# Moving odd-sized tiles to the front of SBUF in a two-layer decoder trunk, so that the streamed tiles start at multiples of 512 bytes

## Chip, cores, metric

One core of a Trainium2 chip runs the whole program. The metric is device time in microseconds from one execution to the next of the same kernel; lower is better.

## What is computed

Two decoder layers on 256 positions of width 2048, all in float32. A layer mixes tokens by two branches that run side by side, adds the result to x, then adds an MLP and a gated per-layer embedding. Cut to what matters:

```python
u = rms_norm(x, g_mix[l])
cq_raw, ckv_raw, xb, yb, gate_a, gate_r = split_columns(u @ w_in[l])
attn = mla_branch(cq_raw, ckv_raw, ...)   # low-rank q and kv, 16 heads, causal softmax
rec = rglru_branch(xb, yb, ...)           # conv of 4 taps, gates by 128x128 blocks, linear scan, gelu(yb) gate
merged = sigmoid(gate_a) * attn + sigmoid(gate_r) * rec
x = x + merged @ w_out[l]
x = x + square(relu(rms_norm(x, g_mlp[l]) @ w_up[l])) @ w_down[l]
x = x + sigmoid(rms_norm(x, g_ple[l]) @ w_ple_gate[l]) * (p[l] @ w_ple_proj[l])
# after both layers: rms_norm(x, g_final)
```

## The kernel before

Everything is kept transposed: features on the 128 partitions, the 256 positions along the free axis. A float32 product is made of three float32r products: each operand is split into a rounded part (hi) and the rest (lo), and TensorE runs hi x hi, hi x lo and lo x hi. So each 128x128 weight tile is worth three matmuls that stream 256 columns.

Weights come from HBM in halves of 128 x 1024 floats, 502 a layer, in the order in which they are used. `load` (line 139) fetches one into a `raw` buffer (six of them), up to eight halves ahead; `split_half` (line 155) has ScalarE write `hi` (line 160) and VectorE write `lo` (line 164), three buffers of each, two halves ahead. Activations are split in the same way: `bufA` and `bufB` hold 16 feature tiles x (hi, lo) x 256 positions, and take turns as input and output of the stages.

TensorE's work is issued by a few helpers. `mm3` (line 257) issues the three products of one weight tile: lines 259, 260 and 261. `mm_both` (line 274) issues a half for two output tiles at once, 24 matmuls, all at line 284; four halves, 96 matmuls, make a pair of output tiles (`mm_pair`). In the trace a matmul is named output <- streamed tile, weight tile: `up<-bufA,hi`.

A layer runs c (compressed q and kv, 8 halves a pair of inputs), kr (rope key, by `mm3` on bufA or bufB), then eight groups of two heads: xb, yb, (in group 0: gr), k, v, q, qr, lru, (from group 1: gr), ga. k, q and qr stream `c1hi`, `c1lo`, `c0hi`, `c0lo`; lru streams the split convolution output; v has c1 as the stationary side and streams `hi` and `lo`. Between the pieces of gr and ga, and of the next group's xb, small blocks run: scores s (lines 259 to 261 and 984), transposes pt (lines 1017 to 1019) and values o (line 1040, on `v` and `pt_hi`, `pt_lo`). Then come out, four chunks of up and down, and pg, with pp (the per-layer embedding's projection) between. The norm's sums (`ms`, line 555) and its spreading (`rb`, line 604) are small matmuls behind the first pieces of a stage.

The order on each engine is set by a planner that runs while the program is built: `work` chooses vector and scalar steps by estimated costs, and `half` and the helpers add up TensorE's time. It knows neither addresses nor pools.

Addresses in SBUF follow from the pools: a pool takes its place behind the pool opened before it, and within one a tile takes its place behind the tile made before it, each rounded up to 32 bytes. The first free byte of a partition is 16,512 (128 past a multiple of 512). Before, `const` comes first, with `x`, `bufA`, `bufB` and then small tiles among large ones; `wraw`, `wsp`, `tmp`, `att` and `tiny` follow.

Of the kernel before, what the change touches and what calls it, by code (L numbers as in the profile page):

```python
# [11 lines left out]
F32 = mybir.dt.float32  # L12
# [6 lines left out]
P = 128  # L19
S = 256  # L20
D = 2048
KT = D // P
DEPTH = 2
# [21 lines left out]
NPC = _c  # L45
# [8 lines left out]
def _parts(x, bits, n):  # L54

    out = []
    x = Fraction(x)
    for i in range(n):
        if x == 0:
            out.append(0.0)  # L60
            continue
        b = bits if i < n - 1 else 24
        m, e = math.frexp(float(x))
        q = Fraction(2) ** (e - b)
        v = Fraction(round(x / q)) * q
        out.append(float(v))
        x -= v
    return out


def _centered(x):
    x = x - math.floor(x)
    return x - 1 if x > Fraction(1, 2) else x
# [3 lines left out]
def trunk_kernel(ctx: ExitStack, tc: tile.TileContext, xT, pT, pos, par, gfin, invf, wu, out):  # L77
    nc = tc.nc

    const = ctx.enter_context(tc.tile_pool(name="const", bufs=1))  # L80
    wraw = ctx.enter_context(tc.tile_pool(name="wraw", bufs=6))
    wsp = ctx.enter_context(tc.tile_pool(name="wsp", bufs=3))
    tmp = ctx.enter_context(tc.tile_pool(name="tmp", bufs=6))
    att = ctx.enter_context(tc.tile_pool(name="att", bufs=1))
    tiny = ctx.enter_context(tc.tile_pool(name="tiny", bufs=4))
    banks = {
        t: (ctx.enter_context(tc.tile_pool(name=f"ps_{t}", bufs=n, space=PSUM)), n)
        for t, n in (("mm", 3), ("s", 2), ("t", 1), ("o", 1), ("r", 1))
# [120 lines left out]
    def later(key, *steps, deps=(), rank=1, also=()):  # L209

        job = Job((key, *also), rank, deps, steps)
        at = len(jobs)
        while at and jobs[at - 1].rank > rank:
            at -= 1
        jobs.insert(at, job)
# [126 lines left out]
        return tmp.tile([P, S], F32, tag="h", bufs=3, name=name)  # L342


    x = const.tile([P, KT, S], F32, name="x")

    bufA, bufB = (const.tile([P, KT, 2, S], F32R, name=n) for n in ("bufA", "bufB"))
    parT = const.tile([P, DEPTH * NPC], F32, name="parT")
    gf = const.tile([P, KT], F32, name="gf")
    nc.sync.dma_start(out=parT, in_=par)  # L350
    nc.sync.dma_start(out=x[:, 0:2, :], in_=xT[:, 0:2, :])
    load_to(0)
# [12 lines left out]
    make_identity(nc, ident)  # L365
    ones = const.tile([P, P], F32, name="ones")
    V.memset(ones, 1.0)
    power = const.tile([P, 4], F32, name="power")
    A.activation(power, ones[:, 0:4], AF.Copy, scale=-0.5)
    mask = const.tile([P, S], F32, name="mask")  # L370
    V.memset(mask[:, 0:P], 0.0)
# [2 lines left out]
    ropeS = const.tile([P, S], F32, name="ropeS")  # L374

    def rope_tables():
        fr = const.tile([P, 1], F32, name="invf")
        nc.sync.dma_start(out=fr, in_=invf)
        slots = []
        for n, tag in enumerate(("xch", "xcl", "vh", "vl")):  # L380
            w = att.tile([P, 512], F32, tag=tag, name=f"rope_w{n}")
            slots += [w[:, 0:S], w[:, S:512]]
        posi, ang, p2, p1, rem, turn, k, k2 = slots
        nc.sync.dma_start(out=posi.bitcast(I32), in_=pos.partition_broadcast(P))
        ops = []

        def ts(*a, **kw):
            ops.append(("V", 0.21, lambda: V.tensor_scalar(*a, **kw)))

        def tt(*a, **kw):  # L390
            ops.append(("V", 0.35, lambda: V.tensor_tensor(*a, **kw)))

        def rounded(o, src, by):
            ts(out=o, in0=src, scalar1=by, scalar2=ROUND, op0=ALU.mult, op1=ALU.add)
            ts(out=o, in0=o, scalar1=ROUND, scalar2=None, op0=ALU.subtract)

        def less(o, src, kk, c):
            ops.append(("V", 0.35, lambda: V.scalar_tensor_tensor(out=o, in0=kk, scalar=-c, in1=src, op0=ALU.mult, op1=ALU.add)))

        ops.append(("V", 0.21, lambda: V.tensor_copy(ang, posi.bitcast(I32))))  # L400
        ts(out=ang, in0=ang, scalar1=fr, scalar2=None, op0=ALU.mult)

        rounded(p2, ang, 2.0 ** -20)
        less(rem, ang, p2, 2.0 ** 20)
        rounded(p1, rem, 2.0 ** -10)
        less(rem, rem, p1, 2.0 ** 10)
        for n, (p, e) in enumerate(((p2, 20), (p1, 10))):
            c = _parts(_centered(Fraction(2) ** e / (2 * _PI)), 12, 3)
            if n == 0:
                ts(out=turn, in0=p, scalar1=c[0], scalar2=None, op0=ALU.mult)  # L410
            else:
                less(turn, turn, p, -c[0])
            rounded(k, turn, 1.0)
            less(turn, turn, k, 1.0)
            less(turn, turn, p, -c[1])
            less(turn, turn, p, -c[2])
        rounded(k, turn, 1.0)
        less(turn, turn, k, 1.0)
        c = _parts(2 * _PI, 12, 3)
        rounded(k2, rem, float(1 / (2 * _PI)))  # L420
        for v in c:
            less(rem, rem, k2, v)
        less(rem, rem, turn, -float(2 * _PI))
        rounded(k, rem, float(1 / (2 * _PI)))
        for v in c:
            less(rem, rem, k, v)
        ts(out=k, in0=rem, scalar1=3.1415925, scalar2=-3.1415925, op0=ALU.min, op1=ALU.max)

        ts(out=k2, in0=k, scalar1=-1.0, scalar2=None, op0=ALU.mult)
        tt(out=k2, in0=k, in1=k2, op=ALU.max)  # L430
        ts(out=k2, in0=k2, scalar1=-1.0, scalar2=math.pi / 2, op0=ALU.mult, op1=ALU.add)
        ops.append(("A", 1.0, lambda: A.activation(ropeS, k, AF.Sin)))
        ops.append(("A", 1.0, lambda: A.activation(ropeC, k2, AF.Sin)))

        for b in (0, 64):
            ts(out=ropeS[b:b + 32, :], in0=ropeS[b:b + 32, :], scalar1=-1.0, scalar2=None, op0=ALU.mult)
        later("rope", *ops, rank=1)


    cl = const.tile([P, DEPTH, 16], F32, name="cl")  # L440
    cl2 = const.tile([P, DEPTH, 16], F32, name="cl2")
    hba = const.tile([P, DEPTH, 16], F32, name="hba")
    hbx = const.tile([P, DEPTH, 16], F32, name="hbx")

    def lru_constants():
        work_ = t512("lru_c")
# [196 lines left out]

    PT = tuple(att.tile([P, 512], F32R, name=f"pt_{w}") for w in ("hi", "lo"))

    xbuf = att.tile([P, 2, 260], F32, name="xbuf")
    V.memset(xbuf[:, :, 0:4], 0.0)

    def split_steps(d, name, src, tag, cols=512):
# [35 lines left out]
    def mixer(l, u, mg, norm):  # L685
# [9 lines left out]
        for n in range(4):  # L695
            i, pr = divmod(n, 2)
            key = ("c", i, pr, l)
            ps = mm_pair(f"c{i}{pr}_{l}", key, u, hooks.get(n, ()))
            later(key, ("A", 0.6, lambda i=i, pr=pr, ps=ps: A.activation(dest(i, pr), ps, AF.Copy)), rank=-1)
            if l == n == 0:  # L700
                rope_tables()
                lru_constants()
            nl.squares((nl.name, "sq", n), lambda i=i, pr=pr: raw[i, pr], i, deps=(key,), last=pr == 1)
# [729 lines left out]
```

## Time and profile before

| | us |
|---|---|
| median of 3 runs | 2882.05 (2879.41 to 2883.55) |
| profiled execution | 2881.91 |
| its span, first to last instruction | 2880.1 |
| TensorE busy | 2853.1 (99%) |
| VectorE busy | 1861.3 (65%) |
| ScalarE busy | 1538.4 (53%) |
| DMA queues, share of 16 engines | 56.1% |

The span lies 1.8 us under the execution's own time. TensorE's share says that it is never long without a matmul, not how fast one follows another: the recorded ends of matmuls are modelled and overlap their successors. The distance from start to start, or a piece of the chain of waits divided by its count, gives the pace.

### The profile page before, as it was taken

The page shows a single profiled execution, that of the slowest core. Times are in us where ns is not written, and L with a number is a line of the kernel's source. Part 1 is how long each engine was busy: PE and PEld are TensorE (multiplying, and loading weights), DVE is VectorE, ACT ScalarE, POOL GpSimd, SP SyncE. Part 2 cuts the span into 40 slices and gives each one's busy share as a digit, 9 for nine tenths or more (in the row PEclk, how much of TensorE's full clock was granted, in tenths as well). Part 3 has the DMA queues.
Part 4 walks back from the last instruction along what each step waited for, and adds up shares of the span by engine and source line. Part 5 has one row for each costly group of instructions (what it writes and reads, how often), then busy time and mean ns, then how long its engine had stood idle before and what let it go on. Part 6 is the DMA issues. An engine that isn't in the chain of part 4 may idle for free.

```text
span 2880.1 us, 60564 instructions
## 1 busy us (share of the span) xinstructions
PE 2853.1 (99%) x24800; PEld 2846.8 (99%) x24800; DVE 1861.3 (65%) x2420; ACT 1538.4 (53%) x2050; POOL 10.1 (0%) x17
## 2 busy tenths in 40 slices
PE   8999999999999999999999999999999999999998
PEld 8999999999999999999999999999999999999998
DVE  7877777765555555556758777777555555555665
ACT  5666666644444443444546666666453444434555
POOL 0000000000000000000000000000000000000000
PEclk9999999999999999999999999999999999999999
DMA  6555555555555555655555555555555555555553
GB/s 232 169 176 179 172 171 178 178 184 190 197 193 194 195 193 195 198 195 191 190 188 172 176 169 176 176 178 179 186 191 195 194 196 193 194 194 197 196 187 129
DMA packets 272583, 535.43 MB, mean 186 GB/s; under 512 B 30512, under 2 KB 30768, under 8 KB 272304
## 3 DMA queue, kind: packets, MB, share of 16 engines
q1 hardware_dynamic: 272304, 531.55, 55.6%
q8 instruction: 194, 3.18, 0.4%
q14 instruction: 85, 0.70, 0.1%
HBM read 529.33 MB, written 2.10 MB: 185 GB/s over the span
## 4 chain that ended last, share of the span: by engine, by line
PE 98%; ACT 1%; DVE 0%; DMA 0%; issue 0%; SPq 0%; ACTq 0%; POOLq 0%
PE up L284 24%; PE down L284 21%; PE yb L284 6%; PE gr L284 6%; PE xb L284 6%; PE out L284 5%; PE pg L284 5%; PE ga L284 5%; PE c L284 3%; PE down L259 1%; PE down L260 1%; PE down L261 1%; PE o L1040 1%; PE s L984 1%; PE v L872 1%; PE v L873 1%
## 5 line engine op out<-in xcount | busy, mean ns | idle before, releaser
L160 ACT ACTIVATE hi<-raw 128x1024 fp32r<-128x1024 f32 x1004 | 1065.7, 1061 | 1311.6 <-DMA raw<-wu 467.4
L164 DVE TENSOR_TENSOR lo<-raw,hi 128x1024 fp32r<-128x1024 f32 x1004 | 1229.5, 1225 | 808.1 <-ACT hi L160 786.0
L284 PE MATMUL up<-bufA,hi 128*128 128x256 f32 x2048 | 316.2, 276 | 0.0
L284 PE MATMUL up<-bufB,hi 128*128 128x256 f32 x2048 | 316.2, 276 | 0.0
L284 PE MATMUL down<-bufB,hi 128*128 128x256 f32 x1792 | 276.0, 276 | 0.0
L284 PE MATMUL down<-bufA,hi 128*128 128x256 f32 x1792 | 276.0, 276 | 0.0
L284 PEld LDWEIGHTS up<-bufA,hi 128*128 128x128 f32 x2048 | 270.6, 188 | 0.1
L284 PEld LDWEIGHTS up<-bufB,hi 128*128 128x128 f32 x2048 | 270.6, 188 | 0.1
L284 PEld LDWEIGHTS down<-bufB,hi 128*128 128x128 f32 x1792 | 236.4, 188 | 0.0
L284 PEld LDWEIGHTS down<-bufA,hi 128*128 128x128 f32 x1792 | 236.4, 188 | 0.0
L284 PE MATMUL up<-bufA,lo 128*128 128x256 f32 x1024 | 199.7, 276 | 0.0
L284 PE MATMUL up<-bufB,lo 128*128 128x256 f32 x1024 | 199.6, 276 | 0.0
L284 PE MATMUL down<-bufA,lo 128*128 128x256 f32 x896 | 174.5, 276 | 0.0
L284 PE MATMUL down<-bufB,lo 128*128 128x256 f32 x896 | 174.4, 276 | 0.0
L284 PEld LDWEIGHTS up<-bufA,lo 128*128 128x128 f32 x1024 | 154.4, 188 | 0.0
L284 PEld LDWEIGHTS up<-bufB,lo 128*128 128x128 f32 x1024 | 154.3, 188 | 0.0
L284 PEld LDWEIGHTS down<-bufA,lo 128*128 128x128 f32 x896 | 134.9, 188 | 0.0
L284 PEld LDWEIGHTS down<-bufB,lo 128*128 128x128 f32 x896 | 134.8, 188 | 0.0
L284 PE MATMUL xb<-bufB,hi 128*128 128x256 f32 x512 | 81.4, 281 | 0.0
L284 PE MATMUL yb<-bufB,hi 128*128 128x256 f32 x512 | 81.3, 281 | 0.0
L284 PE MATMUL yb<-bufA,hi 128*128 128x256 f32 x512 | 81.3, 281 | 0.0
L284 PE MATMUL xb<-bufA,hi 128*128 128x256 f32 x512 | 81.3, 281 | 0.0
(563 smaller groups left out, 5630.8 us busy)
## 6 DMA issues: line engine op xcount, KB each, us to landing
raw<-wu SPq DMA_DIRECT2D x1744, 256.0 KB, 3.0
raw<-wu SPq DMA_DIRECT2D x132, 512.0 KB, 3.3
y<-rows SPq DMA_DIRECT2D x4, 512.0 KB, 4.0
x<-xT SPq DMA_DIRECT2D x3, 512.0 KB, 7.5
x<-xT SPq DMA_DIRECT2D x2, 256.0 KB, 4.3
praw<-pT SPq DMA_DIRECT2D x2, 256.0 KB, 4.0
parT<-par SPq DMA_DIRECT2D x1, 184.0 KB, 2.5
rope_w<-pos SPq DMA_DIRECT2D x1, 128.0 KB, 4.4
```

What stands on the lines that cost most here:

```text
L160: A.activation(hi, src, AF.Copy)
L164: V.tensor_tensor(out=lo, in0=src, in1=f(hi), op=ALU.subtract)
L259: T.matmul(o, lhsT=wh, rhs=ah, start=start, stop=False, skip_group_check=shared)
L260: T.matmul(o, lhsT=wh, rhs=al, start=False, stop=False, skip_group_check=shared)
L261: T.matmul(o, lhsT=wl, rhs=ah, start=False, stop=stop, skip_group_check=shared)
L284: T.matmul(ps[:, t * S:(t + 1) * S], lhsT=w[:, (4 * t + kk) * P:(4 * t + kk + 1) * P], rhs=a, start=k == n == t == 0, stop=k == 15 and n = ...
L872: T.matmul(o, lhsT=ch, rhs=wh, start=k == 0, stop=False)
L873: T.matmul(o, lhsT=ch, rhs=wl, start=False, stop=False)
L984: T.matmul(o, lhsT=qr, rhs=kr["rot"][w][:, 0:n], start=False, stop=m == 1)
L1040: T.matmul(o[:, j * P:S], lhsT=v[:, j * S + t * P:j * S + (t + 1) * P], rhs=q[:, c], start=n == 0, stop=n == 5, skip_group_check=True,)
```

## The change

Two pools are opened ahead of the others, `small` and `even`, and `tiny` is moved between them. The parameter tiles, `gf`, `power`, `invf`, `cl`, `cl2`, `hba`, `hbx` and the convolution's input `xbuf` go from `const` and `att` to `small`. `even` holds one tile of 32 bytes that nothing uses.

```diff
+    small = ctx.enter_context(tc.tile_pool(name="small", bufs=1))
+    tiny = ctx.enter_context(tc.tile_pool(name="tiny", bufs=4))
+    even = ctx.enter_context(tc.tile_pool(name="even", bufs=1))
     const = ctx.enter_context(tc.tile_pool(name="const", bufs=1))
...
-    tiny = ctx.enter_context(tc.tile_pool(name="tiny", bufs=4))
...
+    even.tile([P, 8], F32, name="even")
     x = const.tile([P, KT, S], F32, name="x")
...
-    parT = const.tile([P, DEPTH * NPC], F32, name="parT")
-    gf = const.tile([P, KT], F32, name="gf")
+    parT = small.tile([P, DEPTH * NPC], F32, name="parT")
+    gf = small.tile([P, KT], F32, name="gf")
...
-    power = const.tile([P, 4], F32, name="power")
+    power = small.tile([P, 4], F32, name="power")
...
-        fr = const.tile([P, 1], F32, name="invf")
+        fr = small.tile([P, 1], F32, name="invf")
...
-    cl = const.tile([P, DEPTH, 16], F32, name="cl")
...
+    cl = small.tile([P, DEPTH, 16], F32, name="cl")
...
-    xbuf = att.tile([P, 2, 260], F32, name="xbuf")
+    xbuf = small.tile([P, 2, 260], F32, name="xbuf")
```

`cl2`, `hba` and `hbx` change as `cl` does. The two programs have the same instructions in the same order, with the same waits, on all five engines. What differs is where tiles begin, in bytes of a partition, and the remainder by 512:

| tiles | before | rest | after | rest |
|---|---|---|---|---|
| x | 16,512 | 128 | 20,992 | 0 |
| bufA, bufB | 32,896; 65,664 | 128 | 37,376; 70,144 | 0 |
| ident, ones | 99,968; 100,480 | 128 | 102,912; 103,424 | 0 |
| mask, ropeC, ropeS | from 101,024 | 160 | from 103,936 | 0 |
| norm sums, R | from 104,640 | 192 | from 107,008 | 0 |
| raw (6), hi (3), lo (3) | from 109,760 | 192 | from 112,128 | 0 |
| tmp tiles, pt_hi, pt_lo | from 158,912 | 192 | from 161,280 | 0 |
| xbuf | 178,368 | 192 | 18,592 | 160 |
| other att tiles: xc, v, q, k, c0, c1, kr, qs, p, rec | from 180,448 | 224 | from 180,736 | 0 |
| small tiles, tiny | 98,432 to 104,608; 228,576 | various | 16,512 to 20,960 | various |

Each streamed tile's size is a multiple of 512 bytes; a 128-column weight slice is 512 bytes, a row of bufA 1,024. So the slices of a tile have the tile's remainder. The last byte in use goes from 228,832 to 228,864.

## Rows read from the trace of the kernel before

**Rows 1.** The page's parts 1, 2 and 4: engines, granted clock, chain that ended last.

```profile
PE 2853.1 (99%) x24800; PEld 2846.8 (99%) x24800; DVE 1861.3 (65%) x2420; ACT 1538.4 (53%) x2050; POOL 10.1 (0%) x17
...
PEclk9999999999999999999999999999999999999999
...
PE 98%; ACT 1%; DVE 0%; DMA 0%; issue 0%; SPq 0%; ACTq 0%; POOLq 0%
```

**Rows 2.** The longest pieces of the chain: start us, us, what it was.

```profile
78.82 10.89 PE yb L284 x96
...
140.57 11.31 PE yb L284 x96
163.12 8.18 PE gr L284 x72
...
551.45 79.15 PE out L284 x672
641.91 11.31 PE up L284 x96
...
730.60 76.16 PE down L284 x672
817.64 87.04 PE up L284 x768
...
1926.10 11.31 PE yb L284 x96
```

**Rows 3.** Busy time and granted clock in four stretches: out, down, yb, gr.

```profile
core 0: us, PE busy (x) PEld busy (x) DVE busy (x) ACT busy (x) POOL busy (x), PEclk, DMA share, GB/s
560.00:640.00 80.00, 80.00 (x682) 80.00 (x681) 48.73 (x56) 39.80 (x50) 0.00 (x0) 1.00 0.56 186
740.00:800.00 60.00, 60.00 (x532) 60.00 (x531) 31.26 (x29) 23.39 (x22) 0.00 (x0) 1.00 0.59 195
201.00:212.00 11.00, 11.00 (x95) 11.00 (x95) 8.49 (x12) 5.48 (x7) 0.00 (x0) 1.00 0.58 193
90.00:100.00 10.00, 10.00 (x91) 10.00 (x90) 9.14 (x15) 5.54 (x7) 0.00 (x0) 1.00 0.57 194
```

**Rows 4.** The chain in shorter stretches, 60 to 70 and 137 to 176 us.

```profile
60.43 0.11 PE kr L259
...
65.87 2.72 PE xb L284 x24
...
137.69 2.88 PE xb L284 x24
...
151.88 0.12 PE k L259
...
163.00 0.12 PE lru L261
...
171.29 0.12 PE s L259
...
171.88 0.06 PE s L259
171.94 0.12 PE s L260
172.06 0.11 PE s L261
172.17 0.22 PE s L984 x2
172.39 2.79 PE gr L284 x24
```

**Rows 5.** TensorE's instructions in order of time: start us, us, what, tiles, count.

```profile
start us, us, engine line op out<-in xcount [idle before <-releaser]
...
68.43 0.95 PE L555 MATMUL ms_c<-ones,nacc_c 128*128 128x1 f32 x8
69.23 0.72 PE L284 MATMUL xb<-bufA,hi 128*128 128x256 f32 x4
69.79 0.40 PE L284 MATMUL xb<-bufA,lo 128*128 128x256 f32 x2
...
137.30 0.40 PE L1040 MATMUL o<-pt_lo,v_0h 128*128 128x256 f32 x2
137.53 0.68 PE L284 MATMUL xb<-bufA,hi 128*128 128x256 f32 x4
138.05 0.40 PE L284 MATMUL xb<-bufA,lo 128*128 128x256 f32 x2
```

**Rows 6.** Vector steps of lines 785 and 637 (duration ns min/median/max); who waited, us, times, longest.

```profile
L785 DVE SCALAR_TENSOR_TENSOR xc<-xbuf,parT,xc x96: 475/479/482, 92.4 to 1931.4; 128x256 f32<-128x256 f32 x96
...
L637 DVE SCALAR_TENSOR_TENSOR bufA<-x,parT,bufA x48: 476/480/485, 5.0 to 1342.4; 128x256 fp32r<-128x256 f32 x48
...
ACT hi L160 <- DMA raw<-wu: 467.4, 284, 2.2
...
PE c L284 <- ACT hi L160: 8.6, 1, 8.6
```

More of the change, by code (lines that the diff above doesn't have):

```diff
@@ L437, in rope_tables @@
         later("rope", *ops, rank=1)
-    cl = const.tile([P, DEPTH, 16], F32, name="cl")
-    cl2 = const.tile([P, DEPTH, 16], F32, name="cl2")
-    hba = const.tile([P, DEPTH, 16], F32, name="hba")
-    hbx = const.tile([P, DEPTH, 16], F32, name="hbx")
+    cl = small.tile([P, DEPTH, 16], F32, name="cl")
+    cl2 = small.tile([P, DEPTH, 16], F32, name="cl2")
+    hba = small.tile([P, DEPTH, 16], F32, name="hba")
+    hbx = small.tile([P, DEPTH, 16], F32, name="hbx")
     def lru_constants():
```

## The prediction

> **What bounds the kernel now.** I read the page first: TensorE is busy 99% of the span, its granted clock is full in all 40 slices, and 98% of the chain that ended last is TensorE [rows 1]. The other engines can be late only where TensorE waits for them, and it hardly does. So the question is at what pace TensorE goes from one matmul to the next; for that I read the chain piece by piece and divide a piece's length by its count. Nearly all of the 24,800 matmuls have one form: a 128x128 weight tile, 256 columns streaming, float32r. They do not have one pace. A chunk of the MLP's up projection is 768 matmuls in 87.04 us, down is 672 in 76.16 us: 113.3 ns each, both. The output projection is 672 in 79.15 us: 117.8 ns. Of the y branch, 96 matmuls take 10.89 us in group 0 and 11.31 us in group 1 [rows 2]. The clock is at full, 2.4 GHz, in slow and fast stretches alike. Nor does the other engines' work sort them: the vector engine is busy 61% of the slow out and 52% of the fast down, but 77% of a slow yb and 91% of a fast gr; the DMA share is 0.56 to 0.59 in all four [rows 3]. So there is a **fast pace of 113.3 ns** and a **slow pace of 117.8 ns**, 4.4 ns apart, for the same instruction on the same tiles.
>
> A third observation bears on addresses. The rope-key projection runs the three-matmul helper on bufA (byte 128 of a 512-byte block): 48 matmuls from 60.43 to 65.87 us, 113.3 ns. The same helper on the attention tiles c1, c0 and xc, which begin at byte 224 (v streams the weights instead, with c1 as its stationary side), makes 96 matmuls from 151.88 us to 163.12 us: 117.1 ns [rows 2, 4]. The form is the same and the helper the same, but the tiles lie elsewhere: 128 and 192 are multiples of 64, 224 is not. That is the evidence for the change. It says that a multiple of 64 may be enough, and bufA, bufB, hi and lo, which carry 22,368 of the matmuls (6,144 each in up and down, 1,536 each in xb, yb, gr, ga, out and pg, 768 in c, 96 in kr), have that already.
>
> **What the change removes, adds and moves.** It moves no instruction: on all five engines every row and every wait is the same in both programs. It adds one tile that nobody reads, 32 bytes. All else is addresses, so the costs are those of pace.
>
> 1. Attention and lru matmuls. k, v, q, qr and lru are 96 matmuls in each of 16 groups. At the rope key's pace 96 take 10.88 us; they take 11.24 us: 0.36 us a group, 5.8 us in all. The 192 pp matmuls stream a tile at byte 224 too; no row of mine prices them alone, and at the same 3.7 ns they are worth 0.7 us. The 320 score and 192 value matmuls also read such tiles, but run in bursts of six to ten with half-width ones among them; I bound them between 0 and 2 us (at 4 ns each) and take 1. Sum: 7.5 us, if the address is the cause; nothing, if it is not. All of it is on the path, since TensorE has no slack.
>
> 2. The slow pace on bufA and bufB. It does not go by place: the same loop on the same tiles goes at either pace and stays there until something small comes between. It is entered behind the value matmuls (o, then xb at 137.53 us), whose tiles v and pt lie at bytes 224 and 192, and it then holds for the rest of xb and all of yb; the k block ends it, and gr goes fast [rows 2, 5]. The chain has 26 pieces of 96 at 11.31 us in xb and yb, against 10.89: 26 x 0.42 = 10.9 us. Before them stand 14 pieces of 24 at 2.88 us, against 2.79 for 24 that go fast behind scores [rows 4]: 1.2 us. The last value block of each layer leads into out: 79.15 against 76.16 us for 672, out's last 96 matmuls and up's first 96 at 0.42 each: 3.8 us a layer, 7.7 us in all. Sum: 19.8 us. If the value matmuls, once their tiles lie as bufA does, hand over like the rope key does, this goes; if they hand over as now, it stays. No row decides this, since no value matmul has aligned tiles before. The nearest two disagree: the eight ms matmuls, all of whose tiles lie on multiples of 64, are followed by a slow xb [rows 5], while the kr block, on such tiles and full-width throughout, kept the fast pace and handed it on to xb [rows 4]. I take the gain, as the value matmuls are mostly full-width like kr and not one column like ms, and keep 0 for the range.
>
> 3. The fast pace itself. Half-width score matmuls go at 0.45 us for four, 112.5 ns, though they stream half as much [rows 4]: there the weight load sets the pace, and 113.3 is 0.8 ns above it. If the new addresses take that off too, it is 0.8 ns on 22,368 matmuls: 18 us more. Below nothing, the fast pace could be lost: item S. I take zero.
>
> 4. Vector engine, scalar engine, DMA. The convolution steps read xbuf one, two or three elements off any boundary and take 479 ns; the split of x, at byte 128, takes 480 for the same operation and size [rows 6]. So the vector engine does not see the address. ScalarE waits 467.4 us for weight DMAs, but TensorE does not show as waiting for it beyond the start: quicker landings would end in ScalarE's idle time [rows 6]. Both zero; the cover is the six raw buffers, and only were it gone would some of those 467 us count.
>
> **Sum.** The profiled execution took 2881.91 us, 1.8 over its span, and stands within 0.2 us of the median of the runs (2882.05). 2881.9 - 7.5 - 19.8 = 2854.6, so **2855 us**.
>
> **The rivals.**
> *N, nothing measurable.* It has two forms. In the first the address is no cause, the 3.7 ns have another, and time stays at 2882 us. The row shows 117.1 against 113.3 ns for one form, which speaks against it; that no two tiles were compared at one place in the program speaks for it. The Trainium skill's SBUF — State Buffer (Specifications, and Who interferes with whom) speaks for this form: it gives lines of 16 bytes and says that TensorE waits on no other user of SBUF, and since all starts here are multiples of 32 both before and after, it would have nothing change, 2882 us. By that rule the block from 151.88 us should run at 113.3; the trace does not agree. In the second form the address counts, but the value matmuls still hand over slow. Then the k block, now like bufA, no longer ends the slow pace and inherits it: 96 matmuls at 117.8 in place of 117.1 (14 groups x 0.07 = +0.9 us), gr's 72 at 8.48 in place of 8.18 us (14 x 0.30 = +4.2), against 0.7 us gained in the two groups 0, 0.7 in pp and 1 in scores and values. Net +2.7: 2885 us.
>
> *G, more than forecast.* Items 1 and 2 and the 18 us of item 3: 2837 us. For it: 64 need not be the last boundary that counts, and hi and lo are at odd multiples of 64 today. Against: out and down show that the same addresses already allow 113.3.
>
> *S, slower.* Today weights and stream never start at the same place of a 512-byte block where the pace is fast (192 against 128). After the change they always do. Score matmuls are the only ones with equal starts today (224 and 224), and the five full-width ones from 171.29 us take 0.59 us, 118 ns each [rows 4]. If equal starts are what costs there, the fast pace is lost in up and down: 12,288 matmuls x 4.4 ns = +54 us. With 7.5 us gained elsewhere at most that is 2929 us, and 2960 us if all on bufA and bufB that item 2 does not count (22,368 less 4,560) go slow and nothing is gained. It decides where the first up chunk behind the norm settles: over 115 ns a matmul there, and S holds, since no small matmul comes between to end it for eight chunks. Against it: scores are short bursts, with tiles off the multiple of 64, and may owe their pace to that.
>
> **How the numbers follow.** Forecast 0.36 (2855; 2842 to 2874, as item 2 goes in part), G 0.10 (2837), N 0.29 (2880 to 2886), S 0.25 (2905 to 2960). A measurement of this kernel tells about 0.2%, 5.8 us, from no change. Faster is the forecast and G, 0.46; the same is N, 0.29; slower is S, 0.25. The range runs from 2828, just below G, to 2935, past the 2929 of S; it leaves out some 0.03 below and some 0.12 above. Both signs together are needed to hold eight in ten; the forecast's own range is 2842 to 2874.
>
> **What would show it.** Item 1: the block from k to gr falls from 11.24 to 10.9 us a group. Item 2: the yb pieces fall from 11.31 to 10.89, out from 79.15 to 76.16 us. Item 3: the up chunk stays at 87.04 us; 86.4 would be G, 90.5 S. Second form of N: k to gr near 11.3 and gr at 8.48 instead of 8.18 us. First form: every piece as before. I am wrong at the root if paces change at places where only the addresses of bufA and hi differ from today's while the attention blocks keep theirs; then not the multiple of 64 but the place in 512 bytes, or the distance between the two tiles, is what counts.

## The result: 4.4% slower

The changed kernel takes 3008.05 us (median of 4 runs, 3006.71 to 3008.49) against 2882.8 us: 1.0442 times as long, 95% interval 1.0428 to 1.0455. The forecast was 2855 us with a range of 2828 to 2935 us, so the result lies above it, on the slow side.

The page of the changed kernel, its parts 1, 2 and 4, answers to [rows 1]:

```profile
PE 2980.9 (99%) x24800; PEld 2976.6 (99%) x24800; DVE 1863.2 (62%) x2420; ACT 1537.3 (51%) x2050; POOL 10.2 (0%) x17
...
PEclk9999999999999999999999999999999999999999
...
PE 98%; ACT 1%; DMA 1%; DVE 0%; issue 0%; SPq 0%; ACTq 0%; POOLq 0%; DVEq 0%
```

Nothing is idle that was not idle before. TensorE is busy 99%, at full clock, and makes 98% of the chain, but it takes 2980.9 us for the same 24,800 matmuls that took 2853.1. The chain of the changed kernel (start us, us, what it was), to be held against [rows 2, 4]:

```profile
568.84 80.64 PE out L287 x672
...
754.02 80.64 PE down L287 x672
846.18 92.16 PE up L287 x768
...
146.71 11.52 PE yb L287 x96
158.23 0.12 PE k L262
...
169.75 8.64 PE gr L287 x72
```

Out, down and up now all go at 120.0 ns a matmul (80.64 us / 672; 92.16 / 768), and so do yb (11.52 / 96) and the block from k to gr, from 158.23 to 169.75 us (11.52 / 96). Before, these were 117.8, 113.3, 113.3, 117.8 and 117.1 ns. Both paces of before have gone from these pieces, and one pace, slower than either, holds in all of them. The weight loads show it too. The group of the costliest loads in the kernel before (count | busy us, mean ns of one | idle before):

```profile
L284 PEld LDWEIGHTS up<-bufA,hi 128*128 128x128 f32 x2048 | 270.6, 188 | 0.1
```

and in the changed kernel:

```profile
L287 PEld LDWEIGHTS up<-bufA,hi 128*128 128x128 f32 x2048 | 282.7, 192 | 0.1
```

188 ns became 192 ns. The clock and the other engines do not explain it. A stretch of up in the changed kernel (us; busy time and count of PE, PEld, DVE, ACT and POOL; granted clock, DMA share, GB/s), against [rows 3]:

```profile
850.00:930.00 80.00, 80.00 (x669) 80.00 (x668) 43.33 (x42) 36.49 (x42) 0.00 (x0) 1.00 0.56 183
```

VectorE is busy 54% here and the DMA share is 0.56, as in the stretches of before. Nor do the writes of ScalarE and VectorE into hi and lo make the pace: in this stretch the trace has 665 steps from one matmul's start to the next, and each is 120 ns, whether both of these engines run beside it (127 steps), one of them (460) or neither (78).

Where the 126.6 us of added span lie, piece by piece of the two chains: the eight up chunks 39.4 us, 5.12 each but for the first of a layer, whose start was slow before; the eight down stages 8 x (4.48 + 96 x 6.67 ns) = 41.0; gr in 14 groups, 8.64 for 8.18 us, 6.4; the 26 pieces of xb and yb, 11.52 for 11.31, 5.5; the 16 blocks from k to gr, 11.52 for 11.24, 4.5; out 2 x (1.49 + 0.21) = 3.4. That is 100 us. The rest is mostly pg (9.3 us), c (5.9) and ga (5.0), then gr, xb and yb in the two groups 0 and the short pieces.

### The profile page after: what moved, and what is told of

It is laid out like the page before. It is cut to its first block, busy times and chain, and to the rows that moved or that the text cites. A ratio compares the mean times of both kernels' runs of the same rounds, so it can differ in the third digit from the quotient of the medians.

```text
span 3006.7 us, 60564 instructions
## 1 busy us (share of the span) xinstructions
PE 2980.9 (99%) x24800; PEld 2976.6 (99%) x24800; DVE 1863.2 (62%) x2420; ACT 1537.3 (51%) x2050; POOL 10.2 (0%) x17
## 4 chain that ended last, share of the span: by engine, by line
PE 98%; ACT 1%; DMA 1%; DVE 0%; issue 0%; SPq 0%; ACTq 0%; POOLq 0%; DVEq 0%
PE up L287 25%; PE down L287 21%; PE gr L287 6%; PE yb L287 6%; PE xb L287 6%; PE pg L287 5%; PE out L287 5%; PE ga L287 5%; PE c L287 3%; PE down L264 1%; PE down L263 1%; PE down L262 1%; PE o L1044 1%; PE v L878 1%; PE v L877 1%; PE v L876 1%
## 5 line engine op out<-in xcount | busy, mean ns | idle before, releaser
L287 PE MATMUL up<-bufA,hi 128*128 128x256 f32 x2048 | 329.5, 283 | 0.0
L287 PE MATMUL up<-bufB,hi 128*128 128x256 f32 x2048 | 329.5, 283 | 0.0
L287 PE MATMUL down<-bufB,hi 128*128 128x256 f32 x1792 | 288.1, 283 | 0.0
L287 PE MATMUL down<-bufA,hi 128*128 128x256 f32 x1792 | 288.1, 283 | 0.0
L287 PEld LDWEIGHTS up<-bufA,hi 128*128 128x128 f32 x2048 | 282.7, 192 | 0.1
L287 PEld LDWEIGHTS up<-bufB,hi 128*128 128x128 f32 x2048 | 282.7, 192 | 0.1
L287 PEld LDWEIGHTS down<-bufB,hi 128*128 128x128 f32 x1792 | 247.3, 192 | 0.0
L287 PEld LDWEIGHTS down<-bufA,hi 128*128 128x128 f32 x1792 | 247.3, 192 | 0.0
L287 PE MATMUL up<-bufA,lo 128*128 128x256 f32 x1024 | 206.3, 283 | 0.0
L287 PE MATMUL up<-bufB,lo 128*128 128x256 f32 x1024 | 206.3, 283 | 0.0
```

What stands on the lines that cost most here:

```text
L287: T.matmul(ps[:, t * S:(t + 1) * S], lhsT=w[:, (4 * t + kk) * P:(4 * t + kk + 1) * P], rhs=a, start=k == n == t == 0, stop=k == 15 and n = ...
```

## The experiments

Two theories could explain one pace everywhere. **Distance**: what counts is how far the stream's first byte lies from that of the weight tile, and the change made that distance 0 for every pair. **Absolute place**: a start on a multiple of 512 is itself bad. A third possibility is that something else in the change costs, the move of xbuf and the small tiles above all. In the kernel before the stream lies 64 bytes below its weights for bufA and bufB (128 and 192), 32 above for k, q, qr and lru (224 and 192) and 32 below for v. Below, a distance is stream minus weights, by the remainders by 512.

Every kernel here has the instructions of its base in the same order and differs by where tiles lie: by unused tiles, and in one run by a pool of its own for lo.

**All tiles 32 bytes further, distances still 0.**

```diff
-    even.tile([P, 8], F32, name="even")
+    even.tile([P, 16], F32, name="even")
```

> The changed kernel with the unused tile 32 bytes longer, so that every streamed tile begins at byte 32 of a 512-byte block and none at byte 0; weights and stream still begin at equal remainders. Equal starts cost: all long stages stay at 120.0 ns a matmul (up chunk 92.16 us, out 80.64 us), about 3008 us. Start on a multiple of 512 costs: the paces leave 120 ns, and the time goes towards before, 2883 us. Misalignment to 64 costs (my prediction's reading): slower than 120 ns, over 3008 us.

3007.09 us in one run, beside 2884.08 for the kernel before on the same chip. Its chain:

```profile
566.98 80.64 PE out L287 x672
...
844.32 92.16 PE up L287 x768
```

The same 120.0 ns with every tile at remainder 32. The multiple of 512 is not the cause, and neither is the multiple of 64 that I had read out of the rows.

**Only hi and lo, and what lies behind them, 64 bytes further.**

```diff
     wraw = ctx.enter_context(tc.tile_pool(name="wraw", bufs=6))
+    wpad = ctx.enter_context(tc.tile_pool(name="wpad", bufs=1))
     wsp = ctx.enter_context(tc.tile_pool(name="wsp", bufs=3))
...
     even.tile([P, 8], F32, name="even")
+    wpad.tile([P, 16], F32, name="wpad")
```

> The changed kernel with 64 unused bytes ahead of the split weights hi and lo, and so of all tiles behind them: bufA and bufB at remainder 0, hi, lo and the attention tiles at 64. The distance from weights to stream is -64 for bufA and bufB, as in the kernel before, and 0 for k, q, qr and lru. Equal starts cost: up and down go back to 113.3 ns (87.04 and 76.16 us), while the 96 matmuls from k to gr stay at 120 ns (11.52 us); about 2885 to 2895 us. Absolute start costs: bufA and bufB are on multiples of 512 still, so up stays at 92.16 us and the time near 3008 us. Something else in the change (the small tiles, xbuf, raw) costs: time near 3008 us.

2869.1 us in one run. Its chain:

```profile
548.84 76.16 PE out L288 x672
...
724.13 76.16 PE down L288 x672
811.17 87.04 PE up L288 x768
...
151.99 0.12 PE k L263
...
163.49 8.18 PE gr L288 x72
```

64 unused bytes take back the whole loss: up and down are at 113.3 ns. In the same program the block from k to gr, whose two sides are at 64 and 64, stays at 120 ns (151.99 to 163.49 us, 11.50 us). So the pace goes with the pair. That the small tiles and xbuf stand in front costs nothing that shows. The result is even below the kernel before, which I had not expected: out is at 76.16 us in place of 79.15.

**Only hi and lo, and what lies behind them, 448 bytes further, in the kernel before.** This is the converse: none of the change's moves, but bufA, bufB, hi and lo all at remainder 128.

```diff
+    wpad = ctx.enter_context(tc.tile_pool(name="wpad", bufs=1))
     wsp = ctx.enter_context(tc.tile_pool(name="wsp", bufs=3))
...
+    wpad.tile([P, 112], F32, name="wpad")
     x = const.tile([P, KT, S], F32, name="x")
```

> The kernel before, with 448 unused bytes ahead of hi and lo and nothing else moved in front of them: hi and lo at remainder 128, as bufA and bufB, attention tiles at 160. If equal starts alone make the loss, up and down go to 120.0 ns (92.16 and 80.64 us), the block from k to gr to about 116.7 ns (+32 bytes, as before), and the time to about 3003 us, without any of the change's own moves. If gathering the small tiles, or remainder 0, has a part in it, the time stays well below 3003 us.

3003.15 us, where 3003 was expected. Its chain:

```profile
566.06 80.64 PE out L285 x672
...
843.38 92.16 PE up L285 x768
...
157.62 0.12 PE k L260
...
168.89 8.62 PE gr L285 x72
```

The equal start alone makes the loss. The raw halves stay at 192, as in the kernel before, so their place does not. The block from k to gr, at distance +32 (v at -32), takes 11.27 us, 117.4 ns, close to the 117.1 it had before at the same distances and other addresses.

**Other distances.** Two kernels put bufA, bufB, hi and lo and the attention tiles at four different remainders each. In layer 0 up streams bufA and down bufB; in layer 1 they change places, so each distance is seen in two stages.

```diff
     bufA = const.tile([P, KT, 2, S], F32R, name="bufA")
+    const.tile([P, 8], F32, name="gap")
     bufB = const.tile([P, KT, 2, S], F32R, name="bufB")
...
+    wpad.tile([P, 24], F32, name="wpad")
+    epad.tile([P, 16], F32, name="epad")
```

(`epad` is a pool between `wsp` and `tmp`. The second kernel has 16, 48 and 24 floats for the three.)

> Unused bytes between bufA and bufB, ahead of hi and behind lo: remainders 0 (bufA), 32 (bufB), 128 (hi, lo), 192 (attention tiles), so the distances from weights to stream are -128 with bufA, -96 with bufB, +64 for k, q, qr, lru and -64 for v. In layer 0 up streams bufA and down bufB, in layer 1 the other way. Distance alone counts: up of layer 0 and down of layer 1 share one pace, down of layer 0 and up of layer 1 another, neither of them 120 ns; v at 113.3 or 117.8. Period of 64 bytes in the distance: up of layer 0 (-128) at 120 ns. Absolute remainders count: bufA at 0 keeps 120 ns in up of layer 0 whatever the weights' place.

2961.05 us. The chain, layer 0 and then layer 1, and the start of q and of gr:

```profile
743.25 78.85 PE down L289 x672
833.36 91.14 PE up L289 x768
...
2205.21 79.74 PE down L289 x672
2296.34 90.11 PE up L289 x768
...
161.68 0.11 PE q L264
...
167.12 8.54 PE gr L289 x72
```

At -128 (up of layer 0, down of layer 1) the pace is 118.7 ns, at -96 it is 117.3, and q, qr and lru at +64 go at 113.3 ns (48 from 161.68 to 167.12 us).

> As the run before with other distances: remainders 0 (bufA), 64 (bufB), 256 (hi, lo), 352 (attention tiles): -256 with bufA, -192 with bufB, +96 for k, q, qr, lru and -96 for v. If the distance counts with a period of 128 or 256 bytes, the stages on bufA are at 120.0 ns again (92.16 us for up of layer 0); if its period is 512 or it has none, they are at another pace. Stages on bufB at -192 read as -64 (113.3 ns) by a period of 128.

2983.69 us. Its chain, and the start of q and of gr:

```profile
751.30 79.15 PE down L289 x672
841.76 92.16 PE up L289 x768
...
2222.09 80.64 PE down L289 x672
2314.25 90.45 PE up L289 x768
...
163.41 0.12 PE q L264
...
169.17 8.63 PE gr L289 x72
```

At -256 the pace is 120.0 ns, as at 0. At -192 it is 117.8 ns, the slow one of the two paces seen at -64 in the kernel before. A period of 128 bytes is out, since -128 does not go at the 120.0 ns of 0. And 120.0 ns is not the mark of equal starts alone: q, qr and lru, here at +96, go at that pace too (48 from 163.41 to 169.17 us).

**Distance +64 for everything.** The unused tile goes, hi and lo stand 448 bytes further and the tiles behind them 64 more, as above: bufA, bufB and the attention tiles at 480, hi and lo at 416.

```diff
-    even = ctx.enter_context(tc.tile_pool(name="even", bufs=1))
...
+    wpad = ctx.enter_context(tc.tile_pool(name="wpad", bufs=1))
     wsp = ctx.enter_context(tc.tile_pool(name="wsp", bufs=3))
+    epad = ctx.enter_context(tc.tile_pool(name="epad", bufs=1))
     tmp = ctx.enter_context(tc.tile_pool(name="tmp", bufs=6))
...
-    even.tile([P, 8], F32, name="even")
+    wpad.tile([P, 112], F32, name="wpad")
+    epad.tile([P, 16], F32, name="epad")
```

> The changed kernel without the unused tile and with 448 unused bytes ahead of hi and lo: bufA, bufB and the attention tiles at remainder 480, hi and lo at 416, so the distance is +64 where the 64-byte run had -64. If the size of the distance counts and not its sign, up, down and out go at 113.3 ns, or at 117.8 where they enter it badly, and the block from k to gr near 113.6: 2855 to 2885 us. If the sign counts, another pace: the stages on bufB at -192, which is +64 by a period of 256 bytes, went at 117.8 ns all through, which would make 2955 us.

2944.74 us. Its chain:

```profile
554.81 79.15 PE out L288 x672
...
736.60 79.15 PE down L288 x672
827.05 90.45 PE up L288 x768
...
161.07 0.11 PE q L263
...
166.52 8.16 PE gr L288 x72
```

The sign makes a difference. At +64 out, up and down keep 117.8 ns (90.45 us / 768), where up and down go at 113.3 in every layout at -64. It is the pace of -192, which is +64 less 256; with 0 and -256 that makes two pairs that fit a period of 256 bytes. But in the same program q, qr and lru, also at +64, go at 113.5 ns (161.07 to 166.52 us, 48), and gr behind them, on bufA and bufB at +64, goes at 113.3 (8.16 us / 72). So at either 64 there are two paces, 113.3 and 117.8, and which one holds depends on how the run of matmuls was entered.

**hi at distance 0, lo at distance -64.** lo gets a pool of its own, 64 bytes behind hi's.

```diff
+    lpad = ctx.enter_context(tc.tile_pool(name="lpad", bufs=1))
+    wlo = ctx.enter_context(tc.tile_pool(name="wlo", bufs=3))
...
+    lpad.tile([P, 16], F32, name="lpad")
...
-        lo = wsp.tile([P, 1024], F32R, tag="lo", name=f"lo{h}")
+        lo = wlo.tile([P, 1024], F32R, tag="lo", name=f"lo{h}")
```

> The changed kernel with hi at remainder 0 and lo at 64, bufA and bufB at 0. Of six matmuls in a row four use hi and two lo. If what counts is the weight load that runs beside a stream, so the next matmul's weights, the short gaps follow the fourth and fifth matmul of a six; if it is the matmul's own weights, the fifth and sixth. Without memory from one to the next the mean is (4 x 120.0 + 2 x 113.3) / 6 = 117.8 ns, 2960 us in all; if one equal start keeps the whole series on its grid, 120.0 ns and about 3005 us.

2982.27 us, which neither of the two sums had. A piece of the chain, and TensorE in order of time (start us, us, what, count):

```profile
748.09 79.89 PE down L289 x672
...
760.05 0.64 PE L289 MATMUL down<-bufB,hi 128*128 128x256 f32 x4
760.53 0.40 PE L289 MATMUL down<-bufB,lo 128*128 128x256 f32 x2
```

The matmuls come as four on hi and two on lo, and the down stage is 118.9 ns a matmul, between my 117.8 and 120.0. These rows round to 10 ns; the starts in the trace are kept to the nanosecond. In down's matmuls of line 289 the step from one hi matmul to the next is 120.0 ns on average (2,688 steps), and the steps from hi to lo, lo to lo and lo to hi take 117.5, 118.3 and 117.5 ns on average, 117.8 together (2,688 steps). So three steps of a six are short, where both readings expected two, and they have the slow one of the paces of -64, not 113.3. It is not the two weight tiles alone either: in down's last 96 matmuls, which the three-matmul helper issues as hi, hi, lo, the step from hi to hi takes 117.5 ns. Whether the load that runs beside the stream counts, or the matmul's own weights, stays open.

**Distance 64 everywhere, for use.** The kernel of the 64-byte run with 64 more bytes behind lo: bufA and bufB at 0, hi and lo at 64, attention tiles at 128.

```diff
+    wpad = ctx.enter_context(tc.tile_pool(name="wpad", bufs=1))
     wsp = ctx.enter_context(tc.tile_pool(name="wsp", bufs=3))
+    epad = ctx.enter_context(tc.tile_pool(name="epad", bufs=1))
     tmp = ctx.enter_context(tc.tile_pool(name="tmp", bufs=6))
...
+    wpad.tile([P, 16], F32, name="wpad")
+    epad.tile([P, 16], F32, name="epad")
```

> The changed kernel with 64 unused bytes ahead of hi and lo and 64 more behind them: bufA and bufB at remainder 0, hi and lo at 64, attention tiles at 128, so every long stream lies 64 bytes from its weights, below or above. By the distance theory the 96 matmuls from k to gr go from 120 to about 113.6 ns (10.9 us) and up, down and out stay at 113.3: 2869 less 16 x 96 x 6.4 ns = 9.8 us and about 1 us of pp, 2858 us, 0.8 to 1.0% faster than the kernel before. If the gain of the 64-byte run was chance in how the paces were entered, out goes back to 117.8 ns and the time to 2870 to 2885 us.

2865.76 us (2863.95 to 2866.9) against 2882.41: 0.994 of the time of the kernel before, 95% interval 0.9922 to 0.9958. Its chain:

```profile
548.27 76.16 PE out L289 x672
...
810.62 87.04 PE up L289 x768
...
142.08 10.88 PE yb L289 x96
152.96 0.12 PE k L264
...
155.78 0.12 PE v L880
...
158.52 0.11 PE q L264
...
163.96 8.48 PE gr L289 x72
```

It beats both kernels. Of the expected 11 us over the 64-byte run some 3 came, though that is a single run and the difference little more than the spread. The block from k to gr fell to 11.00 us, as expected, but k itself goes at 117.5 ns (24 from 152.96 to 155.78 us), and gr takes 8.48 us in place of 8.18: it starts at the slow one of its two paces, although q, qr and lru in front of it, at +64, go at 113.3 ns (48 from 158.52 to 163.96 us). The attention tiles moved by 64 bytes against the 64-byte run, and up, down and out kept their 113.3 ns: the place of the tiles behind lo does not set the pace of the long stages.

**Attention tiles at -64 too.** The unused tile goes, hi and lo stand at 32, all else at 480. The pools are those of the kernel at +64, with the two unused tiles of 16 and 112 floats:

```diff
-    even.tile([P, 8], F32, name="even")
+    wpad.tile([P, 16], F32, name="wpad")
+    epad.tile([P, 112], F32, name="epad")
```

> The changed kernel without the unused tile, with 64 unused bytes ahead of hi and lo and 448 behind them: bufA, bufB and the attention tiles at remainder 480, hi and lo at 32, so k, q, qr and lru stream at -64 from their weights, as the long stages do, and v at +64. In the 64-byte run with attention tiles at +64, k went at 117.8 ns and handed gr over at 117.8 in 14 groups. If the pace is handed on as long as the distance stays the same, k stays at 113.3 behind a yb at 113.3 and gr too: 24 x 4.4 + 72 x 4.4 ns in 14 groups, 5.9 us off 2866, so 2860 us. If v at +64 breaks it, gr stays at 8.48 us and the time at 2864 to 2868 us.

2866.64 us (2865.11 to 2867.58) against 2878.48, 0.9955 [0.9938, 0.9972]. Its chain:

```profile
141.75 10.88 PE yb L288 x96
152.63 0.11 PE k L263
...
155.36 0.11 PE v L878
...
158.08 0.12 PE q L263
...
163.73 8.48 PE gr L288 x72
```

k goes at 113.7 ns (24 from 152.63 to 155.36 us), close to the 113.3 of yb in front, since the distance does not change there, and v at +64 is at 113.3 too (2.72 us for 24). But behind v the q block at -64 goes at 117.7 ns (48 from 158.08 to 163.73 us) and gr inherits that: 8.48 us. Here changing the distance and changing it back was enough to land in the slower pace. What is won in k is lost in q.

**In the kernel before, only the attention tiles 480 bytes further.** This asks where the slow out of the kernel before came from.

```diff
     V.memset(xbuf[:, :, 0:4], 0.0)
+    att.tile([P, 120], F32, name="apad")
```

> The kernel before, with 480 unused bytes in the attention pool behind xbuf, so that the attention tiles lie at remainder 192, as hi, lo and the pt tiles do: bufA and bufB keep their -64, k, q, qr, lru, v and the value matmuls get distance 0. The stage paces of the kernel before are entered behind the value matmuls. If the distance inside those decides it, out goes from 79.15 to 76.16 us and most yb pieces from 11.31 to 10.89 us, while the block from k to gr goes from 11.24 to 11.52 us: 2882 less up to 19.8, plus 1536 x 2.9 ns = 4.5, about 2867 us. If it does not, out stays at 79.15 us: 2887 us.

2871.85 us in one run, beside 2878.48. Its chain:

```profile
491.03 11.31 PE xb L284 x96
...
551.50 76.16 PE out L284 x672
...
153.57 0.12 PE k L259
...
165.09 8.19 PE gr L284 x72
```

bufA, bufB, hi and lo have not moved, and out goes from 79.15 to 76.16 us, while the block from k to gr goes to 11.52 us, its price at distance 0. Of the 26 pieces of xb and yb, 19 became fast and 7 did not (11.31 at 491.03 us). So where the attention tiles lie, the value matmuls' operands among them, changes at which pace the next long run starts. It does not decide it alone: the same value matmuls, at the same distance, come before fast and slow pieces in one program.

## Why the prediction was wrong

- **The third observation was read the wrong way.** The rows showed 113.3 ns with tiles at 128 and 192 and 117.1 ns with 224 and 192 [rows 2, 4]. That fits a rule of multiples of 64 and a rule of distances equally well, and I built items 1 and 2 on the first. The first run with all tiles at 32 decides between them: off every multiple of 64, the pace is the same as on a multiple of 512. Item 1's gain of 5.8 us became a loss of 4.5 us.
- **Item 2: the forecast asked whether aligned value matmuls would hand over the fast pace.** There was no fast pace to hand over once bufA and hi stood at distance 0; out took 80.64 us. That the slow pace depends on what comes before, and can go, was right: with bufA and bufB at -64 and the value matmuls' operands moved, out did fall to 76.16 us, in four layouts. The reason given was not: in the last layout but one these operands lie at 480, off every multiple of 64.
- **Rival S had the mechanism and the place, and too small a price.** It said that equal starts would cost, and that the first up chunk would show it over 115 ns. It is 120.0. I priced it at the slow pace already seen, 4.4 ns a matmul, and so got 2929 to 2960 us. The price is 6.7 ns against the fast pace, and even the matmuls that went at the slow pace lost 2.2 ns each. The five score matmuls that I had at distance 0 gave 118 ns; why a burst of five does not show the full price is open. A range whose upper end rests on a pace seen elsewhere is no bound for a configuration that the trace does not hold. S had a chance of 0.25, and the range was cut inside it.
- **N, second form**, predicted that gr would inherit the slow pace of yb and take 8.48 us once k to lru no longer break it. Its 8.48 us came in the two fastest layouts, but by luck: yb goes at 113.3 ns in both, and in one of them the q, qr and lru in front of gr do too.
- **Item 4 held.** The convolution steps that read xbuf take 480 ns at its new place, 479 before, and the median time to landing of a 256 KB half is 3.0 us in both kernels.
- The Trainium skill's SBUF — State Buffer (Who interferes with whom) gives TensorE two independent read ports, one for the stream and one for the weights. By that rule no layout here should differ. The trace does not agree: with neither clock nor work changed, the pace goes from 113.3 to 120.0 ns by the distance between the two operands.

## What to carry to other kernels

When a profile shows one instruction form at two paces, ask for the relation between its operands' addresses before asking for their alignment; rounding every tile to the same boundary fixes that relation for all pairs at once, and here it chose one of the slowest that were tried. Such a test is cheap: an unused tile of 64 bytes between the stream's pool and the weights' pool, and a look at a long stage's pace. The largest effect already in the trace is no upper bound for a layout that the trace does not hold; the range has to reach past it.

## What the runs showed of the hardware

For a 128x128 float32r weight tile and a stream of 256 columns at full clock, in long stages where nothing else is said:

| distance, stream minus weights, bytes | ns a matmul | seen in |
|---|---|---|
| 0 | 120.0 | the changed kernel, all tiles at 32, the kernel before with hi and lo at 128 |
| -256 | 120.0 | bufA, second map |
| -128 | 118.7 | bufA, first map |
| -96 | 117.3 | bufB, first map |
| -64 | 113.3, or 117.8 by how it was entered | the kernel before and four layouts |
| +64 | 117.8; q to lru, and gr behind them, also 113.3 to 113.5 | the layout with +64 everywhere, first map, the fastest layout |
| -192 | 117.8 | bufB, second map |
| +96 | 120.0, in blocks of 48 alone | attention tiles, second map |
| +32, v at -32 | 117.1 and 117.4, in blocks of 96 alone | attention tiles, the kernel before, also with hi and lo at 128 |

The distance counts, with what looks like a period of 256 bytes on the two pairs that were tried, and the absolute place does not (distance 0 gave 120.0 ns at 0, 32 and 128). A run of matmuls keeps the pace it was entered with until something else comes between: in the kernel before out and the first of up, 864 matmuls, at 117.8 ns. That two reads of TensorE get into each other's way by their addresses is what this suggests; no run shows the collision itself, and which weights count, why there are two paces at one distance, and what sets the choice stay open.
